# Row maxima of a windowed attention: products over 64 rows of the key and query tiles, or over all 128

## The chip, the cores and the metric

One core of a Trainium2 chip runs the whole program. The metric is device microseconds of one execution, as a median over several runs.

## The reference

The reference is a trunk of two layers on 1024 latent tokens and 256 context tokens of width 1024. Layer 0 is a state-space mixer beside a convolution; layer 1 is a gated MLP beside a windowed attention, and only the latent stream leaves it. What matters here is the attention of layer 1: 16 query heads in 4 groups, each group with one key and value head of 64 channels, blocks of 128 queries, each block against its own and the two neighbouring blocks of keys, the 256 context keys and a sink logit.

```python
qb = jnp.moveaxis(q.reshape(bsz, nb, W, ATT_KV_HEADS, ATT_REP, ATT_HEAD_DIM), 1, 0)
...
s_lat = jnp.einsum('bqkrd,bskd->bkrqs', qblk, kblk).astype(F32) * ATT_SCALE
s_lat = jnp.where(mblk, s_lat, -jnp.inf)
s_ctx = jnp.einsum('bqkrd,bskd->bkrqs', qblk, k_ctx).astype(F32) * ATT_SCALE
s_snk = jnp.broadcast_to(sink_f, s_ctx.shape[:-1] + (1,))
p = jax.nn.softmax(jnp.concatenate([s_lat, s_ctx, s_snk], axis=-1), axis=-1).astype(vblk.dtype)
```

## The kernel before

All products run on TensorE in float32r, with each operand split into a high and a low part (`split`: ScalarE casts the high part, VectorE or GpSimd subtracts for the low part), so most results are three products: high by high, high by low, low by high (`mm3_`, line 170).

The attention (`attention`, lines 476 to 659) goes through 16 units, each one group of heads (`kv`) and one quarter of the queries (`s`, two blocks of 128). A unit has 9 or 10 steps, one for each tile of 128 keys that a block sees. In each step TensorE gets:

- `att_s`, lines 728 and 729: the scores of a key tile for 4 heads into the tile `st`, as two products. The first is over 128 rows: `ks1` holds the keys' high part in rows 0 to 63 and their low part in rows 64 to 127, and `mv1` holds the queries' high part in both halves. The second is over 65 rows, with the queries' low part and, in row 64, the shift that is subtracted from each score. ScalarE then takes exponentials and casts (731, 738), and VectorE or GpSimd makes the low part `pl` (739).
- `att_pv`, line 746: three products of values and exponentials, of the key tile two steps earlier.
- some columns of other work (`beside`): projections of the next groups' queries and gates (line 170), and later the output projection (line 1009), in the order of the string `REST`.
- up to three pieces of `att_max` for the next unit. A piece is a product of queries and keys, and after it VectorE work on the product: pairs of context products of 256 columns with one maximum (lines 686 and 687), and window products of 384 or 256 columns with a masking copy and a maximum (691, 695 or 697, and 698). There are 4 pairs and 8 window products in a unit, 12 pieces.

`att_max` begins by making `mv1` (ScalarE casts, line 672, one for each half of the rows) and `mv2` (VectorE, line 673). When the 12 pieces are done, VectorE joins the maxima (702 to 708), ScalarE takes an exponential (709), TensorE transposes the result (713), and a DMA on GpSimd's queue (716) puts the shift into row 64 of `mv2`, which line 729 of the next unit reads.

Products of `att_max` rotate over three PSUM banks: `ms` twice, and `m2`. The order on TensorE is the order of the program text (`manual_schedule`); the tile framework's scheduler sets the order on the other engines. `fill` (lines 539 to 555) makes `ks1`, `ks2` and `vs` of the next group one unit before the maxima need them; its line 549 is the VectorE subtraction that writes rows 64 to 127 of `ks1`.

The row maximum only shifts the exponent, and it cancels in the softmax; it need not be exact.

Of the kernel before, what the change touches and what calls it, by code (L numbers as in the profile page):

```python
# [11 lines left out]
PSUM = bass.MemoryType.PSUM  # L12
DRAM = bass.MemoryType.DRAM

P = 128
D = 1024
KT = 8
L = 1024
C = 256
T = L + C  # L20
# [69 lines left out]
def run(steps):  # L90
    """Emit a sequence that is emitted in steps."""
    for _ in steps:
        pass
# [6 lines left out]
# What is done on the tensor engine beside the attention, in this order: projections of queries (q) and gates (g) of a group's  # L100
# two head pairs, both halves of the output projection by token tile (c, d) and their weights (R, W, V); @n: from the n-th unit on.
# [4 lines left out]
# Columns of it for each key tile, by unit of the attention.  # L106
# [3 lines left out]
class Kern:  # L110
# [71 lines left out]
    def mod_half(self, layer, i, pool, prio=0):  # L182
        """Half i % 2 of the weight columns (i // 2)*128.., split."""
        return self.load_w(pool, self.A["modw"][layer, i // 2][:, 4 * (i % 2):4 * (i % 2) + 4], [P, 4, P], "m", prio=prio)
# [4 lines left out]
    def mod_chan_(self, layer, m, dst, pool, plus=0.0, halves=1, bank="mm", ahead=None, raw=None, parts=None):  # L189
        """Columns m*128.. of the modulation, channel-major [P, 2] (latents, context)."""  # L190
        nc = self.nc
        n = 8 // halves
        ps = None
        for h in range(halves):
            if ahead is not None:
                w = ahead.pop(0)
                if 2 * m + h + 2 < 32:
                    ahead.append(self.mod_half(layer, 2 * m + h + 2, pool, 300))
            elif halves == 2:
                w = self.mod_half(layer, 2 * m + h, pool)  # L200
            else:
                w = self.load_w(pool, self.A["modw"][layer, m], [P, 8, P], "w", raw=raw, prio=0, parts=parts)
            if ps is None:
                ps = self.bank(bank) if isinstance(bank, str) else bank
            for j in range(2):
                for k in range(n):
                    nc.tensor.matmul(ps[:4, :P], self.scond[:, n * h + k], w[j][:, k], start=(h + j + k == 0), stop=(h + j + k == halves + n - 1))
        yield 1024
        row = self.const.tile([4, P], F32, name="modrow", tag="modrow", bufs=2)
        nc.vector.tensor_copy(row, ps[:4, :P])  # L210
        yield 0
        nc.tensor.matmul(ps[:, 256:258], row, self.V("sel", 0, 2)[:4], start=True, stop=True)
        nc.vector.tensor_scalar(dst, ps[:, 256:258], self.V(f"modb{layer}", m), plus, op0=ALU.add, op1=ALU.add)

    def gate_rows(self, layer, j, dst, bank="ms"):
        """Gate of one stream broadcast over partitions, [P, D]."""
        nc = self.nc
        for f in range(2):
            pt = self.bank(bank)
            for q in range(4):  # L220
                nc.tensor.matmul(pt[:, q * P:(q + 1) * P], self.gcol[:, layer, 4 * f + q, j:j + 1].broadcast_to([P, P]),
                                 self.ident, start=True, stop=True)
            nc.scalar.copy(dst[:, 512 * f:512 * f + 512], pt)
# [143 lines left out]
    def layer1(self, h1, va_d, e0, free_h1):  # L367
        tc, nc, A = self.tc, self.nc, self.A
        dram = self.dram
        hhi, hlo = h1  # L370
        W = A["wch1"]
# [23 lines left out]
        with ExitStack() as e1:  # L395
            q = e1.enter_context(self.pool(name="kv", bufs=2))
            for f in range(2):
                # keys of two heads of the attention, latents and context
                def ev(ps, a, b):
                    t = q.tile([P, 512], F32, name="kt", tag="kt")  # L400
                    if a == 0:
                        nc.scalar.copy(t[:, :b - a], ps)
                    else:
                        self.rope(q, ps, a, b, t)
                    nc.sync.dma_start(kf_d[2 * f:2 * f + 2, :, a:b].rearrange("k d t -> (k d) t"), t[:, :b - a])

                self.proj_ch(wp, W[24 + f], hhi, hlo, ev, pool_lo=f == 1)
                for t in range(8):
                    ps = self.bank("mm")
                    ts = slice(C + t * P, C + (t + 1) * P)  # L410
                    self.mm3(ps, (lambda k: hhi[:, k, ts], lambda k: hlo[:, k, ts]),
                             (lambda k: wv[k // 2][0][:, k % 2], lambda k: wv[k // 2][1][:, k % 2]), range(8))
                    nc.scalar.activation(vt[:, t, 512 * f:512 * f + 512], ps, AF.Gelu_apprx_tanh)
                wv = None if f else load_v(1)
# [9 lines left out]
    def rope(self, q, ps, a, b, out):  # L424
        """Rotated queries or keys of two heads (128 channels), latents a..b."""
# [65 lines left out]
    def attention(self, wp, W, hhi, hlo, kf_d, va_d, yc_d, gd_d, yd_d, den_d, rd_d, sk_d, ew, free_h1):  # L491
        tc, nc, A = self.tc, self.nc, self.A
        LS = SLICES[:2]
        with ExitStack() as e:
# [44 lines left out]
            def fill(kv):  # L539
                """Stationary forms of one group's keys and values."""  # L540
# [20 lines left out]
            def rest():  # L561
                """What fills the tensor engine beside the attention, with the columns of each step; None while there is nothing to do."""
# [98 lines left out]
    def att_max(self, kv, s, qf, KV, out, u, sk_d):  # L661
        """Stationary-side queries of 2 blocks and the shift of each row."""
# [16 lines left out]
        for b in range(2):  # L679
# [3 lines left out]
            for h2 in range(2):  # L683
                ps = self.bank("ms")
                for h in range(2):
                    nc.tensor.matmul(ps[:, 256 * h:256 * h + 256], mv1[0:64, b, 2 * h2 + h], ks1[0:64, 0:C], start=True, stop=True)  # L686
                nc.vector.tensor_reduce(mx[:, 0, b, 2 * h2:2 * h2 + 2], ps.rearrange("p (h k) -> p h k", h=2), axis=mybir.AxisListType.X, op=ALU.max)
                yield
            for h in range(4):
                ps = self.bank("ms")  # L690
                nc.tensor.matmul(ps[:, :nw], mv1[0:64, b, h], ks1[0:64, C + w0 * P:C + w0 * P + nw], start=True, stop=True)  # L691
# [29 lines left out]
    def att_s(self, KV, mv, b, x, kb, off):  # L721
        """Exponentials of the scores of one key tile, 4 heads, split."""
# [9 lines left out]
        if off:  # L732
            # key j of a neighbouring block, query i: kept where i <= j (before) or i >= j (after)
            nc.gpsimd.affine_select(out=p, in_=p, pattern=[[0, 4], [off, P]], base=0, channel_multiplier=-off,
                                    compare_op=ALU.is_ge, fill=0.0)
# [19 lines left out]
    def out1_open(self, yc_d, wr, raws):  # L755
        """Pools and first half of the last output weight."""
# [9 lines left out]
    def out1_c(self, o, t):  # L766
        """The latent stream's residual plus the gated-MLP half of the output projection."""
# [15 lines left out]
    def out1_den(self, q, den_d, rd_d, sk_d, s, h0=0, h1=16):  # L783
        """Reciprocals of twice the softmax denominators, sinks included, of a quarter of the queries, heads h0..h1."""
# [12 lines left out]
    def out1_next(self, o, qp, wr):  # L797
        """Second half of the last output weight."""
# [10 lines left out]
    def out1_y(self, o, q, yd_d, gd_d, rd_d, t0, n, k0, k1, eng):  # L809
        """Gated attention of tokens t0..t0+n (within a quarter), channel tiles k0..k1, split."""  # L810
# [23 lines left out]
    def out1_mm(self, ps, y, w, f, ks, a=0, i0=0):  # L834
        """Channel tiles ks of the product for one half of the channels."""
# [7 lines left out]
    def out1_ln(self, o, x, ps, t):  # L843
        """Residual and the last layer norm."""
# [23 lines left out]
    def out1_d(self, o, q, ten, t, y0):  # L868
        """The attention's half of the output projection of one token tile."""
# [15 lines left out]
    def out1_d67(self, o, q, ten):  # L885
        """The last quarter: the last group's channels come last."""
# [20 lines left out]
    def conformer(self, cv, csum, e):  # L907
        """silu(layer norm over channels) of the convolution, in place."""
# [38 lines left out]
    def split_wo(self, wo, raws, slots, vec=None):  # L947
        """Split one half of an output weight; low parts go to free slots and to those of the values loaded for the tiles before."""
# [17 lines left out]
    def load_wo(self, wo, wr, src, pool_lo=(), more=(), raws=()):  # L966
        """One half (8 K tiles) of an output weight, split; raws are loaded already, the next ones land in the slots of more."""
# [19 lines left out]
    def out_mm(self, ob, src, w, parts=None, by_k=False):  # L987
        """Token tile of an output projection half: two PSUM banks."""
# [23 lines left out]
    def ln_mv(self, q, t):  # L1012
        """mean and rstd over the free dimension."""
# [10 lines left out]
    def ln_stats(self, q, t):  # L1024
        """mean and rstd as scale and bias columns."""
# [118 lines left out]
    def proj_last_(self, wp, src, hhi, hlo, evac, slices, pool_lo=False):  # L1144
        """The low part of the activations is done with first."""
# [22 lines left out]
    def inproj0(self, hhi, hlo, cv, xbc_d, zs_d, gs_d, dtr, vwh, yb_d, xt_d, hb_d, s0, first):  # L1168
# [100 lines left out]
        def token_major(xq, c, h):  # L1269
            """x and B of half a chunk, tokens on partitions."""  # L1270
# [63 lines left out]
    def dt_prep(self, dtr):  # L1334
        """dt, decays and running sums of both directions, [P, dir, chunk, head]."""
        tc, nc, A = self.tc, self.nc, self.A
        cst = self.s0
        with ExitStack() as e:
# [56 lines left out]
            # rows of three exact float32r parts: running sums in head order, biases as (position in quad, quad)  # L1395
# [23 lines left out]
    def ssd_back(self, xt_d, hb_d):  # L1419
        """The state entering each chunk from behind."""  # L1420
# [39 lines left out]
    def rstd_of(self, var, out, scale=1.0):  # L1460
        """out = (var * scale + eps) ** -0.5"""
# [7 lines left out]
class SsdFwd:  # L1469
    """Forward half of the scan and the output of one chunk."""  # L1470
# [6 lines left out]
    def prep(self):  # L1477
        """Loads, the state for the next chunk, C^T B and the diagonal's coefficients."""
# [42 lines left out]
    def mix(self):  # L1521
        """The chunk's output from its own positions and from both states."""
# [43 lines left out]
    def finish(self):  # L1566
        """Gate by z, the RMS statistic, channel-major store."""
# [32 lines left out]
```

## Time and profile before

| | |
|---|---|
| median of 3 runs | 2266.37 us (2262.7 to 2266.95) |
| profiled execution, first to last instruction | 2267.6 us |
| granted TensorE clock, mean of the span | 0.970 |
| attention with its maxima, 1591 to 2107 us | 516 us, of it TensorE busy 502.8, VectorE 319.1, ScalarE 301.0, GpSimd 213.9 |
| from there to the end | 160.6 us, TensorE busy 139.3 |

The profiled execution has no other time than its span; it lies 1.2 us above the median. A row of a timeline gives the start, the duration, the engine, the line, the operation, the names and the shape. In a shape such as `64*128 64x384` the first pair is rows by columns of the array that the weights take, the second is rows by columns of the operand that streams through. Matmuls overlap their neighbours, so the price of one in a stream is the distance from its start to the next one's start, not its duration. PEld is the load of a matmul's weights.

### The profile page before, as it was taken

The page shows a single profiled execution, that of the slowest core. Times are in us where ns is not written, and L with a number is a line of the kernel's source. Part 1 is how long each engine was busy: PE and PEld are TensorE (multiplying, and loading weights), DVE is VectorE, ACT ScalarE, POOL GpSimd, SP SyncE. Part 2 cuts the span into 40 slices and gives each one's busy share as a digit, 9 for nine tenths or more (in the row PEclk, how much of TensorE's full clock was granted, in tenths as well). Part 3 has the DMA queues.
Part 4 walks back from the last instruction along what each step waited for, and adds up shares of the span by engine and source line. Part 5 has one row for each costly group of instructions (what it writes and reads, how often), then busy time and mean ns, then how long its engine had stood idle before and what let it go on. Part 6 is the DMA issues. An engine that isn't in the chain of part 4 may idle for free.

```text
span 2267.6 us, 28582 instructions
## 1 busy us (share of the span) xinstructions
PE 2148.1 (95%) x10748; PEld 1647.3 (73%) x10748; DVE 1470.1 (65%) x1912; ACT 1005.1 (44%) x1553; POOL 1015.7 (45%) x652
## 2 busy tenths in 40 slices
PE   7998998889999999999999999999999999899997
PEld 6877876769997766656789788888666666666676
DVE  6799999988743377677775133223665566566677
ACT  4355565543552233333333233325556666545510
POOL 0088998870223355444330128433344444424453
PEclk9999999989999999899999999999999999899998
DMA  7121111115535765555434224323112111523363
GB/s 271 57 67 57 42 51 64 63 59 170 180 113 191 249 194 176 169 192 180 140 115 134 75 77 170 128 84 98 51 45 60 31 45 53 161 83 116 111 187 128
DMA packets 160145, 262.79 MB, mean 116 GB/s; under 512 B 19028, under 2 KB 98768, under 8 KB 159752
## 3 DMA queue, kind: packets, MB, share of 16 engines
q1 hardware_dynamic: 158584, 257.45, 34.9%
q0 software_dynamic: 1280, 3.26, 0.5%
q8 instruction: 84, 1.38, 0.2%
q14 instruction: 53, 0.43, 0.1%
q10 hardware_dynamic: 144, 0.26, 0.0%
HBM read 186.55 MB, written 74.32 MB: 115 GB/s over the span
## 4 chain that ended last, share of the span: by engine, by line
PE 58%; DVE 7%; DMA 5%; ACT 3%; issue 2%; POOL 2%; SPq 0%; POOLq 0%; DVEq 0%; ACTq 0%
PE m L170 28%; PE m L1009 12%; PE po L746 4%; PE st L728 2%; PE st L729 1%; PE ms L691 1%; DMA mr<-in_modw_dram 1%; PE m L840 1%; PE po L1542 1%; DVE ml L158 1%; PE ms L686 1%; ACT rb L433 1%; POOL ks L828 1%; PE m L691 1%; PE yd L1563 1%
## 5 line engine op out<-in xcount | busy, mean ns | idle before, releaser
L170 PE MATMUL m<-hhi,wh 128*128 128x512 f32 (+1 forms) x840 | 306.9, 369 | 36.8 <-ACT pad L1235 35.2
L1216 POOL TENSOR_TENSOR accq<-accq,prod 128x1295 f32<-128x1295 f32 x90 | 319.0, 3545 | 43.7 <-ACT prod L1215 30.3
L170 PE MATMUL m<-hlo,wh 128*128 128x512 f32 (+1 forms) x840 | 308.2, 367 | 0.0
L170 PE MATMUL m<-hhi,wl 128*128 128x512 f32 (+1 forms) x840 | 306.1, 365 | 1.0 <-DVE wl L158 1.0
L1224 DVE SCALAR_TENSOR_TENSOR acc<-u,vwh,acc 128x1295 f32<-128x1295 f32 x150 | 234.8, 1565 | 6.1 <-issue 2.2
L739 POOL TENSOR_TENSOR pl<-pt,ph 128x512 fp32r<-128x512 f32 x96 | 129.0, 1344 | 236.7 <-ACT ph L738 227.7
L170 PE MATMUL m<-h1hi,wh 128*128 128x512 f32 (+1 forms) x544 | 218.3, 401 | 2.0 <-ACT rb L433 1.4
L170 PE MATMUL m<-h1lo,wh 128*128 128x512 f32 (+1 forms) x544 | 217.0, 399 | 0.0
L170 PE MATMUL m<-h1hi,wl 128*128 128x512 f32 (+1 forms) x544 | 216.3, 398 | 0.0
L170 PEld LDWEIGHTS m<-hhi,wh 128*128 128x128 f32 x840 | 161.7, 194 | 64.4 <-ACT pad L1235 38.3
L1009 PE MATMUL m<-woh,yh 128*128 128x512 f32 x448 | 187.0, 421 | 0.6 <-ACT yh L157 0.2
L1009 PE MATMUL m<-wol,yh 128*128 128x512 f32 x448 | 185.3, 414 | 1.0 <-DVE wol L158 0.5
L1009 PE MATMUL m<-woh,ylo 128*128 128x512 f32 x448 | 185.0, 413 | 0.5 <-DVE ylo L158 0.5
L170 PEld LDWEIGHTS m<-hhi,wl 128*128 128x128 f32 x840 | 162.6, 194 | 27.9 <-issue 3.4
L170 PEld LDWEIGHTS m<-hlo,wh 128*128 128x128 f32 x840 | 163.0, 194 | 24.6 <-issue 2.4
L1215 ACT ACTIVATE prod<-u,vwh 128x1295 f32<-128x1295 f32 x90 | 123.4, 1378 | 82.0 <-POOL accq L1216 81.9
L738 ACT CAST ph<-pt 128x512 fp32r<-128x512 f32 x152 | 93.1, 619 | 115.3 <-PE po L746 107.9
L158 POOL TENSOR_TENSOR wl<-wr,wh 128x1024 fp32r<-128x1024 f32 x33 | 80.6, 2443 | 122.7 <-ACT wh L157 99.0
L1244 DVE SCALAR_TENSOR_TENSOR acc<-pad,vecs,acc 128x1282 f32<-128x1282 f32 x48 | 131.8, 2748 | 3.2 <-issue 1.8
L170 PEld LDWEIGHTS m<-h1hi,wh 128*128 128x128 f32 x544 | 103.2, 190 | 28.7 <-issue 2.6
L746 PE MATMUL po<-ph,vs 128*66 128x512 f32 x304 | 122.9, 404 | 0.8 <-ACT ph L738 0.8
L731 ACT ACTIVATE pt<-st 128x512 f32<-128x512 f32 x152 | 90.7, 597 | 74.2 <-PE st L729 54.5
(360 smaller groups left out, 4890.2 us busy)
## 6 DMA issues: line engine op xcount, KB each, us to landing
wr<-in_wch_dram SPq DMA_DIRECT2D x69, 512.0 KB
mr<-in_modw_dram SPq DMA_DIRECT2D x64, 256.0 KB
mr<-in_modw_dram SPq DMA_DIRECT2D x16, 512.0 KB
wor<-in_wout_dram SPq DMA_DIRECT2D x16, 512.0 KB
xcT<-xbc_d SPq DMA_DIRECT2D x20, 320.0 KB
xt_d<-xtok SPq DMA_DIRECT2D x20, 320.0 KB
xtok<-xt_d SPq DMA_DIRECT2D x10, 640.0 KB
xt<-xt_d SPq DMA_DIRECT2D x10, 640.0 KB
```

The lines of the kernel that those rows point to most:

```text
L158: (nc.gpsimd if pool_lo else nc.vector).tensor_tensor(lo, src, hi.bitcast(F32), op=ALU.subtract)
L170: nc.tensor.matmul(out, x(k), y(k), start=(c == 0), stop=(c == tot - 1))
L691: nc.tensor.matmul(ps[:, :nw], mv1[0:64, b, h], ks1[0:64, C + w0 * P:C + w0 * P + nw], start=True, stop=True)
L731: nc.scalar.activation(p.rearrange("p h t -> p (h t)"), ps, AF.Exp, scale=0.125)
L738: nc.scalar.copy(ph, p)
L739: (nc.gpsimd if x in (0, 1, 3) else nc.vector).tensor_tensor(pl, p, ph.bitcast(F32), op=ALU.subtract)
L746: nc.tensor.matmul(po[:66], vs[:, kb, v], p[y], start=first and i == 0, stop=last and i == 2)
L1009: nc.tensor.matmul(ps[f], y[u][:, k], w[k][v][:, 512 * f:512 * f + 512], start=i + j == 0, stop=i + j == 9)
L1215: nc.scalar.activation(pr, u[:, k:k + N], AF.Copy, scale=vwh[:, i, k:k + 1])
L1216: nc.gpsimd.tensor_tensor(acc, acc, pr, op=ALU.add)
L1224: nc.vector.scalar_tensor_tensor(acc[:, :N], u[:, k:k + N], vwh[:, i, k:k + 1], acc[:, :N], op0=ALU.mult, op1=ALU.add)
L1244: nc.vector.scalar_tensor_tensor(acc, pad[:, k:k + N], w(k), acc, op0=ALU.mult, op1=ALU.add)
```

## The change

Both products of `att_max` use all 128 partitions of `mv1` and `ks1` instead of the first 64. The product is then of the queries' high part with the keys' high and low parts together. The rest of the diff removes comments and docstrings.

```diff
-                    nc.tensor.matmul(ps[:, 256 * h:256 * h + 256], mv1[0:64, b, 2 * h2 + h], ks1[0:64, 0:C], start=True, stop=True)
+                    nc.tensor.matmul(ps[:, 256 * h:256 * h + 256], mv1[:, b, 2 * h2 + h], ks1[:, 0:C], start=True, stop=True)
...
-                nc.tensor.matmul(ps[:, :nw], mv1[0:64, b, h], ks1[0:64, C + w0 * P:C + w0 * P + nw], start=True, stop=True)
+                nc.tensor.matmul(ps[:, :nw], mv1[:, b, h], ks1[:, C + w0 * P:C + w0 * P + nw], start=True, stop=True)
```

The order on TensorE and on SyncE's queue is the same in both kernels. The scheduler places some instructions differently on VectorE (in five places), on ScalarE (two) and on GpSimd (one). On VectorE, in the middle of one unit's maxima (masking copies 697, maxima 698, beside them the rotation of projected queries, 434), the difference is:

```order
 L697 COPY_PREDICATED m_14916<-mk,low 128x2x128
 L739 TENSOR_TENSOR pl<-pt,ph 128x512
-L697 COPY_PREDICATED ms<-mk,low 128x2x128
 L698 TENSOR_REDUCE mxs<-m_14916 128x1
-L698 TENSOR_REDUCE mxs<-ms 128x1
-L434 TENSOR_TENSOR rb<-rb,rope 128x512
+L697 COPY_PREDICATED ms<-mk,low 128x2x128
+L434 TENSOR_TENSOR rb<-rb,rope 128x512
+L698 TENSOR_REDUCE mxs<-ms 128x1
```

The masking copy of one product moves behind the maximum of the product before it, and the rotation moves ahead of the next maximum.

On VectorE at the head of another unit's maxima (context maxima 687 beside a low part of exponentials, 739) it is:

```order
 L739 TENSOR_TENSOR pl<-pt,ph 128x512 x2
 L673 TENSOR_TENSOR mv_16665<-qf,mv_16664 64x2x128 x4
-L687 TENSOR_REDUCE mxs<-ms 128x2
-L739 TENSOR_TENSOR pl<-pt,ph 128x512
-L687 TENSOR_REDUCE mxs<-ms 128x2
+L739 TENSOR_TENSOR pl<-pt,ph 128x512
+L687 TENSOR_REDUCE mxs<-ms 128x2 x2
```

The low part goes ahead of the first context maximum instead of between the two.

## Rows read from the trace of the kernel before

**Rows 1.** The page, part 1: busy us, share of the span, instructions.

```profile
PE 2148.1 (95%) x10748; PEld 1647.3 (73%) x10748; DVE 1470.1 (65%) x1912; ACT 1005.1 (44%) x1553; POOL 1015.7 (45%) x652
```

**Rows 2.** Waits of PE, 1590 to 2120 us: us in total, times, longest us.

```profile
PE ms L713 <- ACT mpack L709: 2.7, 1, 2.7
PE po L746 <- DVE pl L739: 2.5, 3, 2.0
PE ms L686 <- ACT mv L672: 1.3, 3, 0.5
```

**Rows 3.** Lines 686 and 691: times, ns min/median/max, first and last start, shapes.

```profile
L686 PE MATMUL ms<-ks,mv x88: 271/379/579, 1591.4 to 2101.1; 64*128 64x256 f32 x88
L686 PE MATMUL m<-ks,mv x40: 271/380/579, 1621.1 to 2061.8; 64*128 64x256 f32 x40
...
L691 PE MATMUL ms<-ks,mv x84: 379/437/686, 1595.2 to 2105.3; 64*128 64x384 f32 x64, 64*128 64x256 f32 x20
L691 PE MATMUL m<-ks,mv x44: 380/437/686, 1594.0 to 2106.3; 64*128 64x384 f32 x32, 64*128 64x256 f32 x12
```

**Rows 4.** Timeline of PE around a context pair: start us, us, instruction.

```profile
1811.61 0.40 PE L729 MATMUL st<-mv,ks 65*128 65x512 f32 x1
1811.85 0.40 PE L170 MATMUL m<-h1hi,wl 128*128 128x512 f32 x1
1812.18 0.49 PE L686 MATMUL ms<-ks,mv 64*128 64x256 f32 x2
1812.60 0.50 PE L170 MATMUL m<-h1hi,wh 128*128 128x512 f32 x1
1812.94 0.39 PE L170 MATMUL m<-h1lo,wh 128*128 128x512 f32 x1
```

**Rows 5.** Timeline of PE around a window product.

```profile
1816.20 0.39 PE L170 MATMUL m<-h1hi,wl 128*128 128x512 f32 x1
1816.53 0.44 PE L691 MATMUL ms<-ks,mv 64*128 64x384 f32 x1
1816.90 0.50 PE L170 MATMUL m<-h1hi,wh 128*128 128x512 f32 x1
1817.23 0.39 PE L170 MATMUL m<-h1lo,wh 128*128 128x512 f32 x1
```

**Rows 6.** Timeline of PE where full-height products of 256 columns follow each other.

```profile
1230.43 0.28 PE L170 MATMUL m<-wvh,h1lo 128*128 128x256 f32 x1
1230.55 0.28 PE L170 MATMUL m<-wvh,h1hi 128*128 128x256 f32 x1
```

**Rows 7.** VectorE by line and shape, 1590 to 2110 us: busy us, mean ns | idle before.

```profile
L698 DVE TENSOR_REDUCE mxs<-ms 128x1 f32<-128x384 f32 x64 | 34.6, 550 | 0.6
L697 DVE COPY_PREDICATED_SCALAR ms<-mk,low 128x256 f32 x64 | 30.9, 484 | 16.0 <-PE ms L691 14.9
L687 DVE TENSOR_REDUCE mxs<-ms 128x2 f32<-128x512 f32 x44 | 30.2, 685 | 15.6 <-PE ms L686 15.5
```

**Rows 8.** Seven of 16 units, first to last product of the maxima, and the sum of 16. Columns: stretch, its us, busy us (and count) of PE, PEld, DVE, ACT, POOL, granted clock, DMA share, GB/s.

```profile
1591.06:1605.99 14.93, 14.93 (x52) 8.28 (x51) 12.88 (x28) 8.76 (x17) 5.31 (x4) 1.00 0.41 116
...
1647.74:1664.97 17.23, 17.02 (x59) 9.21 (x58) 14.57 (x25) 9.21 (x18) 6.18 (x6) 1.00 0.22 69
...
1741.51:1765.61 24.10, 23.05 (x59) 12.01 (x58) 14.58 (x27) 13.32 (x26) 7.55 (x6) 0.72 0.13 31
1778.76:1796.72 17.96, 17.37 (x59) 9.43 (x58) 14.62 (x27) 12.99 (x24) 8.40 (x7) 1.00 0.14 38
...
1873.23:1891.49 18.26, 17.38 (x59) 9.16 (x57) 14.96 (x29) 13.13 (x28) 6.34 (x5) 1.00 0.18 46
...
2051.99:2070.39 18.40, 18.40 (x67) 10.45 (x65) 14.72 (x29) 7.95 (x14) 4.15 (x5) 1.00 0.22 67
2088.80:2106.94 18.14, 18.14 (x66) 10.38 (x65) 16.61 (x31) 8.12 (x16) 8.30 (x7) 1.00 0.40 127
sum 290.37, PE 282.43 PEld 157.71 DVE 217.68 ACT 157.44 POOL 97.16; mean PE 17.65 PEld 9.86 DVE 13.61 ACT 9.84 POOL 6.07
```

## The prediction

> **What bounds the kernel now.** I read the page first: TensorE is busy for 95% of the span, VectorE for 65%, the others for under half [rows 1]. The change touches only products of the attention's maxima, so the next view is the waits of TensorE in that stage. In some 520 us its waits for other engines come to a few microseconds: 2.7 at the first unit's transpose, 2.5 for low parts of exponentials, 1.3 for the queries' casts [rows 2]. TensorE bounds this stage, and a microsecond taken from its stream there is a microsecond of the span until another engine becomes the bound. What follows the attention (the output projection's last part) waits for the attention's end, so it shifts and does not shrink.
>
> Being busy says nothing about whether the stream is dense, so I then read starts in the timeline, around a product of each touched kind. In a plain stretch one product of 512 columns starts 0.23 to 0.24 us after the one before it; the 65-row product of the scores does so too, from 1811.61 to 1811.85 [rows 4]. Full-height products of 256 columns start 0.12 us apart [rows 6]. Around a pair of 64-row products it is different: from the plain product at 1811.85 to the pair it takes 0.33 us, the pair takes 0.42, and the plain product behind it needs 0.34 until the next starts [rows 4]. A window product alone shows the same: 0.33, 0.37, 0.33 [rows 5]. So TensorE pays on the way into the 64-row products, in them, and on the way out.
>
> **The change, part by part.**
>
> *Height of the products.* It takes 256 products in 192 visits: 128 context products in 64 pairs (88 and 40) and 128 window products (84 and 44) [rows 3]; 12 visits in each of 16 units. The price of a visit comes from the starts. The pair: 1812.94 - 1811.85 = 1.09 us [rows 4]. The same columns at full height and plain spacing: 0.23 + 0.12 + 0.12 + 0.23 = 0.70. Difference 0.39. The window product: 1817.23 - 1816.20 = 1.03 us [rows 5]; plain, with 384 columns halfway between 256 and 512, 0.23 + 0.175 + 0.23 = 0.64. Difference again 0.39. If full height removes the whole difference, TensorE's stream gets shorter by 192 x 0.39 = 75 us, 4.7 us in each unit.
>
> Does full height remove it? The trace of before has no full-height product at this place, but its neighbours bound it. Rows of 128 and of 65 both run at plain spacing [rows 4], so it is not the height as an amount of work, nor a wait on a semaphore as such: the score product also waits for others and costs nothing extra. From below, the gain is nothing if the loads of these weights are slow for another reason; from above it is 75. I take the whole 75, because the new products have the very operands of line 728 (`mv1` and `ks1`, 128 rows), with their roles swapped.
>
> [...]
>
> *What VectorE lets through.* Each piece asks VectorE for a context maximum (685 ns) or a masking copy and a maximum (484 + 550 ns) [rows 7]. With TensorE 4.7 us faster in a unit, VectorE may not follow. In the 16 stretches from first to last product VectorE is busy for 217.7 of 290.4 us [rows 8]. Unit by unit, a stretch cannot become shorter than VectorE's work in it, unless that work runs on past the last product. The room (stretch minus VectorE) is under 4.7 us by a clear margin in six units: 2.1, 2.7, 3.3, 3.3, 3.7 and 1.5 us, in the order of the rows, with 1741.51 left out [rows 8]. Those six give 16.6. The ten others at 4.7 give 47. Together 63.6 us. That is the sum if nothing trails; 75 is the sum if all of VectorE's surplus trails into the stretch after the last product, where TensorE has about as much time again before the next unit and VectorE has little to do. Three PSUM banks let a product run ahead of VectorE by up to three pieces, so some of it will trail. I take 66.
>
> *The new waits.* The products now also wait for the second half of `mv1` (one more cast, line 672, in front of a pair) and for `ks1`'s low half (line 549). The first is bounded by nothing (the casts are done when TensorE arrives) and by one cast for each of 16 units at what the existing wait costs now, up to 0.5 us each [rows 2], 8 us. TensorE waits there only 3 times today, so I take 1 us. Behind a waiting product stand the scores and the value products of the running unit, as TensorE goes in order. The second I take at nothing: `fill` runs one unit ahead of the maxima, and in the first unit the products read the context keys first; if that cover were gone, it would be one subtraction once in each of four groups.
>
> *The order on VectorE.* The moved copies, maxima and rotations are the same instructions; they cost nothing while VectorE has room. A low part that stands behind a maximum can make the value products wait, as it does for 2.5 us now [rows 2]. That is why I stay well below 75.
>
> Sum: 66 - 1 = 65 us less. The profiled execution has 2267.6 us, the median is 1.2 lower; 2267.6 - 65 - 1.2 = **2201 us**.
>
> **The rivals.**
>
> *VectorE takes half of it back.* If VectorE's work packs badly, each unit ends with about 2 us in which TensorE waits for it (a masking copy and a maximum of the last pieces, 2 x 1.03 us [rows 7]). Then 16 x 2 = 32 us fall off the 63.6, less 1 for the casts: gain 30, time 2235. For it: six units where VectorE has hardly room [rows 8]. Against it: VectorE idles for 15 us each before lines 687 and 697, waiting for TensorE [rows 7], which a faster TensorE gives back.
>
> *More than the sum.* One unit ran at a granted clock of 0.72 and took 24.1 us where its like take 17 to 18 [rows 8]. If that stretch, some 6.5 us, is not repeated and all of the 75 comes, with up to 4 us of the small waits [rows 2] gone, the gain is about 85 and the time 2181.
>
> *Nothing changes.* If the extra time belongs to the place (weights that change at each product, banks that are freed late) and not to the height, the starts stay as they are and the time is 2266. For it: nothing in the starts but that no full-height product stands exactly there. Against it: rows 4. [...]
>
> [...]
>
> **How the numbers follow.** Forecast (gain 55 to 78) 0.68; half taken back 0.13; more than the sum 0.13; nothing 0.04; slower 0.02. The likeliest is 2201. The range reaches from 2180 (more than the sum) to 2235 (half taken back) and leaves out nothing, slower and the far ends of these two, some 0.15. A measurement of this kernel can tell 0.2% from no change, 4.5 us. Faster by more than that: 0.94, within it 0.04, slower 0.02.
>
> **What would show it.** Right: starts around a visit at plain spacing (0.23, 0.12 or about 0.18), 16 stretches that sum to about 225 us instead of 290, VectorE busy for 90% and more of them, small new waits of TensorE on lines 687, 697, 698 and 739, and an unchanged 160 us behind the attention. Wrong on the height: distances of 0.33 and 0.37 stay. Wrong on VectorE: distances are plain, but waits of 1 us and more stand before lines 686 and 691. Wrong on the clock: stretches below 0.9 granted clock in more than two units.

## The result, and the profile after

The changed kernel takes 2207.45 us (median of 4 runs, 2205.72 to 2211.47) against 2264.53 of the kernel before (4 runs, 2257.74 to 2266.95): ratio 0.9754, 95% interval 0.9727 to 0.9781, 57 us faster. The forecast was 2201, in a range from 2180 to 2235. The profiled execution has a span of 2203.9 us, 63.7 less than the one before. Part of that difference is the granted clock of the execution profiled before (0.970): of 31 further runs of that kernel the four at a mean granted clock of 0.979 or more took 2255.5 to 2258.7 us, the three at 0.971 or less 2266.7 to 2271.1.

The whole forecast hung on the starts of TensorE's products. Here is the timeline of TensorE in the changed kernel around a context pair and around a window product, the same places of the program as [rows 4, 5]:

```profile
1781.22 0.40 PE L729 MATMUL st<-mv,ks 65*128 65x512 f32 x1
1781.45 0.40 PE L170 MATMUL m<-h1hi,wl 128*128 128x512 f32 x1
1781.68 0.40 PE L686 MATMUL ms<-ks,mv 128*128 128x256 f32 x2
1781.92 0.40 PE L170 MATMUL m<-h1hi,wh 128*128 128x512 f32 x1
1782.16 0.39 PE L170 MATMUL m<-h1lo,wh 128*128 128x512 f32 x1
...
1784.65 0.40 PE L170 MATMUL m<-h1hi,wl 128*128 128x512 f32 x1
1784.88 0.34 PE L691 MATMUL ms<-ks,mv 128*128 128x384 f32 x1
1785.06 0.40 PE L170 MATMUL m<-h1hi,wh 128*128 128x512 f32 x1
1785.29 0.39 PE L170 MATMUL m<-h1lo,wh 128*128 128x512 f32 x1
```

The distances were 0.33, 0.42 and 0.34 us around the pair and are now 0.23, 0.24 and 0.24; around the window product 0.33, 0.37 and 0.33 became 0.23, 0.18 and 0.23. Twice as many rows are multiplied, and the 0.39 us extra of a visit are gone to a hundredth or two.

The loads of the weights (PEld) show where these 0.39 us sat. The first three lines are the loads around the window product of [rows 5] in the kernel before, the last is the load of the window product above in the changed kernel:

```profile
1816.53 0.18 PEld L691 LDWEIGHTS ms<-ks,mv 64*128 64x128 f32 x1 [0.36 <-DVE ms L697]
1816.89 0.19 PEld L170 LDWEIGHTS m<-h1hi,wh 128*128 128x128 f32 x1 [0.19 <-issue]
1817.00 0.19 PEld L170 LDWEIGHTS m<-h1lo,wh 128*128 128x128 f32 x1
...
1784.65 0.19 PEld L691 LDWEIGHTS ms<-ks,mv 128*128 128x128 f32 x1
```

In the changed kernel the load starts together with the product before its own (1784.65) and runs under it; its own product starts at 1784.88. At a change of height it does not: the load for the 64-row product starts only with that product (1816.53), and so does the load for the first 128-row product behind it (1816.89, the product at 1816.90). In the trace of before this is so at all 192 ways into a visit and all 192 ways out; in the changed kernel 393 of the 448 loads at these places start with the product before, the others later, most of them where TensorE waits. The profile puts the idle time before the first load down to VectorE's copies (697), but the changed kernel has the same copies and no such time. Two loads of 0.18 to 0.19 us in the open are about the price of a visit. That they are its cause is argued from their places and sizes: no run changed a load alone.

Next, the 16 stretches from first to last product of a unit's maxima, columns as in [rows 8], the same seven units and the sum of 16:

```profile
1592.28:1604.00 11.72, 10.99 (x52) 8.39 (x51) 11.59 (x26) 8.80 (x17) 5.11 (x3) 1.00 0.42 117
...
1640.03:1654.14 14.11, 12.60 (x59) 9.48 (x58) 13.51 (x23) 9.13 (x18) 5.52 (x5) 1.00 0.22 65
...
1722.23:1737.57 15.34, 12.72 (x60) 9.48 (x58) 12.85 (x25) 12.57 (x24) 7.21 (x6) 1.00 0.21 49
1751.53:1766.27 14.74, 13.16 (x59) 9.56 (x58) 13.25 (x24) 12.83 (x24) 7.87 (x6) 1.00 0.09 18
...
1834.78:1850.18 15.40, 12.95 (x59) 9.28 (x57) 14.13 (x28) 12.41 (x27) 6.63 (x5) 1.00 0.21 54
...
1993.97:2008.22 14.25, 14.00 (x66) 10.88 (x65) 13.62 (x27) 7.97 (x14) 3.89 (x5) 1.00 0.22 57
2027.91:2044.07 16.16, 14.59 (x66) 10.37 (x65) 15.90 (x30) 8.14 (x16) 7.58 (x6) 1.00 0.47 142
sum 225.29, PE 206.09 PEld 157.74 DVE 201.51 ACT 152.34 POOL 91.41; mean PE 12.88 PEld 9.86 DVE 12.59 ACT 9.52 POOL 5.71
```

The stretches went from 290.4 to 225.3 us, 65.1 less. VectorE is now busy for 201.5 of 225.3 us, 89%; it was 75% before. What lies between these stretches took 225.5 us before and takes 226.5 now, and what follows the attention 160.7 and 159.8: nothing was gained or lost there. So the change acted in the maxima and nowhere else.

Last, what TensorE waits for in this stage (1590 to 2060 us; us in total, times, longest), all waits of 1 us and more:

```profile
PE po L746 <- DVE pl L739: 5.5, 5, 2.0
PE m L221 <- DVE gdt L533: 5.0, 1, 5.0
PE ms L686 <- ACT mv L672: 4.9, 8, 1.1
PE po L746 <- POOL pl L739: 4.5, 4, 1.7
PE ms L713 <- ACT mpack L709: 2.7, 1, 2.7
PE m L691 <- DVE mxs L698: 1.7, 5, 0.7
PE po L746 <- ACT ph L738: 1.7, 2, 1.2
PE m L170 <- ACT rb L433: 1.4, 1, 1.4
PE m L713 <- ACT mpack L709: 1.3, 2, 0.7
```

Beside the three lines of [rows 2] the kernel before had a wait of 0.8 us for exponentials (738) and these two, the first of them the longest of its stage:

```profile
PE m L221 <- DVE gdt L533: 4.7, 1, 4.7
PE po L746 <- POOL pl L739: 0.9, 2, 0.6
```

The wait for VectorE's low parts grew from 2.5 to 5.5 us, that for the queries' casts from 1.3 to 4.9, that for GpSimd's low parts from 0.9 to 4.5; waits of line 691 for a bank are new, and the wait of line 221 stays as it was. All of TensorE's waits in the stage come to 12.9 us before and 29.6 now; by the engine that ended last, VectorE's grew by 5.7 us, ScalarE's by 7.4 and GpSimd's by 3.6. VectorE's side shows the reverse (busy us, mean ns | idle before):

```profile
L697 DVE COPY_PREDICATED_SCALAR ms<-mk,low 128x256 f32 x64 | 30.0, 477 | 2.2 <-PE ms L691 2.0
L687 DVE TENSOR_REDUCE mxs<-ms 128x2 f32<-128x512 f32 x44 | 29.9, 682 | 3.5 <-PE ms L686 3.2
```

Its idle time before these two lines was 16.0 and 15.6 us [rows 7] and is 2.2 and 3.5. There TensorE hardly keeps it waiting any more.

### The profile page after: what moved, and what is told of

Its sections match the earlier page's. It is cut to its first block, busy times and chain, and to the rows that moved or that the text cites. A ratio compares the mean times of both kernels' runs of the same rounds, so it can differ in the third digit from the quotient of the medians.

```text
span 2203.9 us, 28585 instructions
## 1 busy us (share of the span) xinstructions
PE 2060.6 (93%) x10748; PEld 1637.6 (74%) x10748; DVE 1467.6 (67%) x1912; ACT 1002.4 (45%) x1553; POOL 1016.9 (46%) x652
## 4 chain that ended last, share of the span: by engine, by line
PE 52%; DVE 10%; DMA 5%; ACT 5%; issue 3%; POOL 2%; SPq 0%; POOLq 0%; DVEq 0%; ACTq 0%
PE m L170 25%; PE m L1009 11%; PE po L746 3%; PE st L729 1%; PE st L728 1%; PE po L1542 1%; PE m L840 1%; ACT rb L433 1%; ACT mv L672 1%; DVE ml L158 1%; DMA mr<-in_modw_dram 1%; PE sg L1553 1%; POOL ks L828 1%; PE yd L1563 1%; DMA vs<-rd_d 1%
## 5 line engine op out<-in xcount | busy, mean ns | idle before, releaser
L170 PE MATMUL m<-h1hi,wh 128*128 128x512 f32 (+1 forms) x544 | 212.6, 391 | 1.9 <-ACT rb L433 1.4
L170 PE MATMUL m<-h1hi,wl 128*128 128x512 f32 (+1 forms) x544 | 211.8, 390 | 0.0
L170 PEld LDWEIGHTS m<-h1hi,wl 128*128 128x128 f32 x544 | 102.4, 188 | 21.0
```

The source lines that it names most:

```text
L170: nc.tensor.matmul(out, x(k), y(k), start=(c == 0), stop=(c == tot - 1))
```

## The experiments

**One row more than 64.** The products use 65 rows, without the other 63 rows of the keys' low part.

```diff
-    nc.tensor.matmul(ps[:, :nw], mv1[:, b, h], ks1[:, C + w0 * P:C + w0 * P + nw], start=True, stop=True)
+    nc.tensor.matmul(ps[:, :nw], mv1[0:65, b, h], ks1[0:65, C + w0 * P:C + w0 * P + nw], start=True, stop=True)
```

(and the context products likewise)

> The maxima's products use rows 0 to 64 (65 rows) instead of all 128, so the keys' low part is left out but for one channel. Theory (a product of more than 64 rows is issued as a full-height one, and only the height counts): starts around a visit at 0.23, 0.12 and 0.18 us, the time within 6 us of the changed kernel's 2207. Rival (what counts is how much of the array is filled, or what the products compute): distances near those of 64 rows, a time near 2264. Rival (the new placement on VectorE made the gain): the distances stay long and the time goes with VectorE's order.

2206.89 us (4 runs), ratio 0.9746, interval 0.9727 to 0.9766: the same as at 128 rows. The timeline around a pair:

```profile
1778.79 0.40 PE L746 MATMUL po<-ph,vs 128*66 128x512 f32 x1
1779.02 0.41 PE L686 MATMUL m<-ks,mv 65*128 65x256 f32 x2
1779.27 0.40 PE L170 MATMUL m<-h1lo,wh 128*128 128x512 f32 x1
```

Starts are 0.23 and 0.25 us apart. What the other 63 rows compute plays no part; 65 rows are enough. The sum of the 16 stretches is 225.05 us, against 225.3 at 128 rows. The rival that VectorE's new order made the gain is not settled by this run; the kernel before without masking copies (below) leaves it no room, as 58 us less of VectorE's work gain nothing there.

**Half of the change, either half.** First the window products alone at full height (line 691), then the context pairs alone (line 686).

```diff
 # e2: of the kernel before, line 691 alone
-    nc.tensor.matmul(ps[:, :nw], mv1[0:64, b, h], ks1[0:64, ...], start=True, stop=True)
+    nc.tensor.matmul(ps[:, :nw], mv1[:, b, h], ks1[:, ...], start=True, stop=True)
 # e3: of the kernel before, line 686 alone
-    nc.tensor.matmul(ps[:, ...], mv1[0:64, b, 2 * h2 + h], ks1[0:64, 0:C], start=True, stop=True)
+    nc.tensor.matmul(ps[:, ...], mv1[:, b, 2 * h2 + h], ks1[:, 0:C], start=True, stop=True)
```

> Only the 128 window products have full height; the 64 context pairs keep 64 rows. Theory (0.39 us a visit, each visit on its own): two thirds of the visits go, 50 of 75 us in TensorE's stream, and two thirds of the measured 57 us in the time, 2226. Rival (VectorE bounds the maxima and takes the rest): alone the window products meet less of the limit, so more than two thirds comes, 45 us or more, 2219 or less, and the two halves add up to clearly more than 57.

> Only the 64 context pairs have full height; the window products keep 64 rows. Theory (each visit on its own): one third of 57 us, 2245. Rival (VectorE bounds the maxima): 22 us or more, 2242 or less, and the sum with the other half is clearly more than 57 us. Neighbouring visits of both kinds (a pair, one plain product, a window product) should each keep or lose their own 0.39 us.

Window products alone: 2228.42 us, ratio 0.9843 (0.9822 to 0.9865). Context pairs alone: 2239.14 us, ratio 0.9892 (0.9865 to 0.9919). Against 2264.27 of the kernel before on the same chip these are 36 and 25 us. The two halves together give 61, the whole change 57. The intervals are some 5 us wide to each side, so the theory's 38 and 19 and the rival's "clearly more than 57" are not told apart by these times; the window products' 36 us fall short of the rival's 45, the pairs' 25 exceed its 22. The 16 stretches sum to 243.6 and 265.6 us, against 290.4 before and 225.3 with both: 46.8 and 24.8 less alone, 65.1 together and not 71.6. Half of these 6.5 us of overlap is the clock: the unit of [rows 8] at a granted clock of 0.72 counts its loss in both halves (5.5 us), and one stretch of the first half ran at 0.89 (2.4 us the other way). The 14 other units overlap by 3.3 us, as they must if other engines begin to hold TensorE up. In a unit that nothing else holds, the parts add up. This is the unit at 1811.85, which took 16.54 us before and takes 11.86 with both, with the window products alone and with the pairs alone at full height:

```profile
1789.26:1802.65 13.39, 13.39 (x59) 9.32 (x58) 10.67 (x23) 8.59 (x16) 6.05 (x5) 1.00 0.23 70
1793.86:1808.85 14.99, 14.99 (x59) 9.39 (x58) 10.97 (x23) 8.70 (x16) 6.61 (x6) 1.00 0.20 62
```

3.15 and 1.55 us less are eight and four visits at 0.39, and both together take off 4.68. The units at 1712.12 and 2018.90 show the same to 0.05 us.

**Twice the product in one visit.** The kernel before with each window product issued twice; the output is the same.

```diff
     nc.tensor.matmul(ps[:, :nw], mv1[0:64, b, h], ks1[0:64, C + w0 * P:C + w0 * P + nw], start=True, stop=True)
+    nc.tensor.matmul(ps[:, :nw], mv1[0:64, b, h], ks1[0:64, C + w0 * P:C + w0 * P + nw], start=True, stop=True)
```

> The kernel before with each 64-row window product issued twice in a row, with the same result. It prices what happens inside a visit. Theory (only the change of height costs, on the way in and out): the second product starts some 0.18 us after the first, the time grows by 128 x 0.18 = 23 us. Rival (between 64-row products the weights are not loaded under the running product either, as 0.42 us for a pair lets one think): 0.28 us, 36 us.

The timeline around one such visit (line numbers behind 691 are one higher):

```profile
1815.51 0.39 PE L170 MATMUL m<-h1hi,wl 128*128 128x512 f32 x1
1815.84 0.44 PE L691 MATMUL ms<-ks,mv 64*128 64x384 f32 x1
1816.12 0.33 PE L692 MATMUL ms<-ks,mv 64*128 64x384 f32 x1
1816.38 0.50 PE L170 MATMUL m<-h1hi,wh 128*128 128x512 f32 x1
1816.71 0.40 PE L170 MATMUL m<-h1lo,wh 128*128 128x512 f32 x1
```

The second product does start 0.28 us after the first, as the rival said, but the next plain product then follows 0.26 us behind and not 0.37. From 1815.51 to 1816.71 it is 1.20 us; a visit with one product took 1.03 [rows 5]. The second product adds 0.17 us, its plain price. In all 96 visits with products of 384 columns the two distances are these to 0.01 us. In sum the theory holds: the visit has a price, not the product. The time, one run of 2275.25, is 11 us above the kernel before where 23 were expected; the runs of the kernel before beside it lie 9 us apart, so a single run prices nothing, and the starts decide.

**Fewer visits, the same products.** If that is so, the kernel before can be helped at 64 rows: two window products next to each other, so that their 128 visits become 64.

```diff
     nc.vector.tensor_reduce(mx[:, 1, b, h:h + 1], ps[:, :nw], axis=mybir.AxisListType.X, op=ALU.max)
-    yield
+    for _ in range(2 * (h % 2)):
+        yield
```

> The kernel before, all products at 64 rows, but the window products issued two and two next to each other: 64 visits fewer, the same products. Theory (a visit costs 0.39 us whatever is in it, for the two changes of height): 64 x 0.39 = 25 us less, 2240. Rival (each 64-row product pays for itself, because its weights are not loaded under a running product): starts of 0.28 to 0.37 us for each, at most 6 us gained.

2240.32 us (4 runs), ratio 0.9887 (0.9863 to 0.9912), 24 us faster than 2264.05 of the kernel before beside it. This is the cleanest test of the price in the time: no product changed its height, none was left out, and 64 visits fewer gave 24 us where 25 were expected and the rival allowed 6. The interval reaches from 20 to 31 us, so that they agree to 1 us is luck. The pieces come in other steps of a unit, so the order of TensorE's work shifts a little and the stretches cannot be set against those of before. In its trace 128 visits are left, and a visit with two products of 384 columns has the distances of the one above (0.33, 0.28, 0.26 and 0.33 us).

**VectorE relieved, at either height.** The masking copies are left out, so the row maxima are taken over the whole window.

```diff
-    a, n = int(w0 == B), (w0 < B) + (w1 > B)
-    edge = ps[:, :P] if w1 == B else ...
-    if n == 1:
-        nc.vector.copy_predicated(out=edge, mask=mk[:, a], data=self.low.broadcast_to([P, P]))
-    else:
-        nc.vector.copy_predicated(out=edge, mask=mk, data=self.low.unsqueeze(2).broadcast_to([P, 2, P]))
     nc.vector.tensor_reduce(mx[:, 1, b, h:h + 1], ps[:, :nw], axis=mybir.AxisListType.X, op=ALU.max)
```

> The changed kernel (128 rows) without the masking copies of the maxima (lines 693 to 697): the row maximum is then taken over the whole window, masked keys included, which only shifts the exponent. VectorE loses 96 x 0.48 + 32 x 0.35 = 58 us of work, TensorE nothing. Theory (what the 16 stretches of maxima still have above TensorE's plain 196 us, 225 - 196 = 29, is mostly VectorE): the stretches fall to about 208 us and the time by 12 to 18 us, to 2192. Rival (the casts of the queries on ScalarE, or the chain of exponentials, hold the rest): less than 5 us, 2203 or more.

> The same without masking copies in the kernel before (64 rows). Theory (there TensorE's bubbles bound the maxima and VectorE had room): nothing to gain, within 5 us of 2264, while the same edit gains 12 to 18 at 128 rows. Rival (VectorE's work costs the same in both): the same gain as at 128 rows, 2250.

At 128 rows 2197.08 us (5 runs), ratio to the kernel before 0.9696 (0.9672 to 0.9719), where the changed kernel, run once more (below), has 0.975 (0.9728 to 0.9771): some 10 to 12 us faster than the changed kernel. At 64 rows 2262.06 us (10 runs), ratio 0.9982 (0.996 to 1.0003), no difference that the runs can tell; 12 of its 16 stretches are the same as before to 0.1 us. So VectorE holds a part of the maxima at 128 rows and none at 64. But the gain is under the 12 to 18 expected. The sum of the stretches and the waits of TensorE in the stage at 128 rows without masks (line numbers behind 691 are six lower):

```profile
sum 218.97, PE 203.75 PEld 159.32 DVE 167.86 ACT 148.74 POOL 89.29; mean PE 12.73 PEld 9.96 DVE 10.49 ACT 9.30 POOL 5.58
```

```profile
PE ms L686 <- ACT mv L672: 4.8, 8, 1.1
PE po L740 <- POOL pl L733: 4.7, 4, 2.2
PE m L221 <- DVE gdt L533: 4.7, 1, 4.7
PE po L740 <- ACT ph L732: 3.6, 2, 2.4
PE po L740 <- DVE pl L733: 2.5, 4, 1.1
```

Three of the six units that had little room, those at 1640.03, 1751.53 and 1834.78 in the changed kernel:

```profile
1631.15:1645.23 14.08, 12.55 (x60) 9.55 (x59) 11.84 (x18) 9.15 (x18) 5.53 (x5) 1.00 0.23 66
1740.84:1755.14 14.30, 12.89 (x60) 9.62 (x58) 11.44 (x19) 12.39 (x24) 7.96 (x6) 1.00 0.07 13
1823.61:1838.47 14.86, 12.66 (x58) 9.35 (x57) 12.03 (x22) 11.88 (x26) 6.11 (x5) 1.00 0.21 56
```

VectorE falls to 168 us in the stretches, the stretches only from 225 to 219 and not to 208. The waits for VectorE's low parts go from 5.5 to 2.5 us, those of line 691 from 1.9 to 0.2, and the one for the transpose (line 713, 4.0 us) is gone; those for ScalarE's casts and for GpSimd's low parts stay. The three units had 14.11, 14.74 and 15.40 us and lose 0.0, 0.4 and 0.5, although VectorE now has 2 to 3 us to spare in each: something else held them, and in these three TensorE waits for the queries' casts, 0.7, 1.4 and 1.7 us with the masking copies and 0.7, 1.4 and 1.6 without. What the stretches have above TensorE's own 196 us (an estimate: the columns of their products at 0.23 us for 512) is thus VectorE's for a part only. The rest is a mixture of ScalarE, GpSimd and the one wait of line 221, which stood there before the change.

**The second cast, on another engine.** Twice: on GpSimd, in the changed kernel, and on VectorE, in the kernel without masks.

```diff
-    for r in range(2):
-        nc.scalar.copy(mv1[64 * r:64 * r + 64, :, 2 * i + hh], src)
+    nc.scalar.copy(mv1[0:64, :, 2 * i + hh], src)
+    nc.gpsimd.tensor_copy(mv1[64:128, :, 2 * i + hh], src)   # e9: nc.vector
```

> The changed kernel with the second half of the queries' tile (rows 64 to 127) cast by GpSimd instead of ScalarE, 64 casts of 0.42 us taken off ScalarE. It is about the new wait: context pairs now wait for both halves, and waits on line 672 went from 1.3 to 4.9 us. Theory (the second cast in front of the pair is the wait): these waits go back to about 1 us, the time to 2203. Rival (GpSimd's casts stand behind its low parts of 1.3 us, and the pair waits for them instead): the wait moves to GpSimd, the time stays or is some us longer, 2207 to 2213.

> The 128-row kernel without masking copies, and the second half of the queries' tile cast by VectorE, which has the room now, instead of ScalarE: 27 us of work change sides. Theory (in the units with the longest stretches, 14 to 15 us, ScalarE is busy for 12 to 13 and holds TensorE at line 672): the waits on line 672 go from 4.8 to 2 us or less, the sum of the stretches from 219 to about 213, the time to 2191. Rival (the chain of exponentials holds these units, not the casts): waits move to line 746, the time stays at 2197 or more.

On GpSimd 2215.53 us (4 runs, 2212.08 to 2221.95), ratio 0.9783 (0.9754 to 0.9812): some 8 us slower than the changed kernel, and beyond what either side expected. The wait of the pairs did go, from 4.9 us to 0.7 on GpSimd's cast:

```profile
sum 233.50, PE 212.33 PEld 162.79 DVE 208.73 ACT 127.92 POOL 106.33; mean PE 13.27 PEld 10.17 DVE 13.05 ACT 8.00 POOL 6.65
```

```profile
PE po L746 <- DVE pl L739: 9.8, 6, 2.7
...
PE ms L686 <- POOL mv L672: 0.7, 2, 0.4
```

The stretches are 8 us longer all the same: VectorE is busier by 7 us for the same instructions (its subtraction for `mv2` takes 700 ns on average instead of 606), and its low parts come later. There is a second reason, which this run does not separate from the first: five stretches of its profile have a granted clock of 0.83 to 0.90, where the changed kernel has one below full clock. The two that grew most, by 3.3 and 2.5 us, both stand at 0.90. On VectorE it is 2206.17 us, ratio 0.9735 (0.9711 to 0.9759), 9 us slower than without that move. The waits on line 672 are gone here too, but the sum of the stretches is 225.4 us, not 213. One row tells much of why; line, operation and shape, busy us, mean ns | idle before:

```profile
L672 DVE CAST mv<-qf 64x256 fp32r<-64x256 f32 x60 | 38.9, 649 | 18.7 <-PE st L722 17.2
```

VectorE stands still for 17 us before these casts, until the scores of the unit before have read the buffer that they write, and the maxima queue behind it: line 691 now waits for context maxima, 4.0 and 3.6 us, and line 746 for VectorE's low parts 5.8 instead of 2.5. Four of its stretches were granted 0.89 to 0.96, against two at 0.93 and 0.95 without the move, so here too the clock has a part that is not separated. In this kernel the casts are better off on ScalarE, by some 8 and 9 us, although TensorE waits for them.

**The changed kernel once more.**

> The changed kernel once more, beside the kernels above on the same chip, so that the gains are taken from runs of one place: 2207, ratio 0.975.

2206.9 us (5 runs), ratio 0.975 (0.9728 to 0.9771), and 223.6 us for the sum of the stretches. The fastest kernel of the study is the one without masking copies at 128 rows, 2197.08 us.

## Why the prediction was right

**Height of the products: right.** 192 visits at 0.39 us, 75 us of TensorE's stream, were said to go whole, and the distances are now plain ones in the pair, in the window product and behind both. That the price belongs to the visit is shown three ways: 65 rows pay nothing (2206.89 us), two products in a visit pay once (the second adds 0.17 us), and with 64 visits fewer the time falls by 24 us. What the prediction left open ("if the loads of these weights are slow") is answered by the loads: they are no slower than others (0.18 to 0.19 us), but at all 384 changes of height in the trace of before they start with their own product, where in a plain stretch they start 0.23 us ahead of it.

**What VectorE lets through: right in the sum, only partly in the cause.** The unit-by-unit sum was 63.6 us, the forecast 66 less 1. The profiles' stretches differ by 65.1. The six units with little room were given 16.6 us and gained 18.5 (3.2, 3.1, 3.2, 2.9, 4.2 and 2.0); the ten others were given 47 and gained 46.6. Four things behind these numbers were not as argued. Four of the ten others had less room than 4.7 us too (4.3, 4.0, 4.2 and 4.4), so the rule taken strictly gives 61.7. VectorE's work did run on past the last products, as I had supposed: between the stretches it is busy for 110.8 us instead of 101.3, and these took 226.5 us instead of 225.5, so it cost next to nothing. 8.8 of the 46.6 come from one unit, the one at a granted clock of 0.72 before and at full clock after; without its 4 us above the price of twelve visits the ten others would have stayed at 42.5.

And VectorE was not the engine that held most of the rest: without its masking copies three of the six units with little room kept 14.1, 14.3 and 14.9 of their 14.1, 14.7 and 15.4 us. What is missing from 75 is the 17 us by which TensorE's waits grew, 7.4 of them for ScalarE, 5.7 for VectorE and 3.6 for GpSimd (1.3 of ScalarE's, at the transpose, hang on VectorE's maxima, as the run without masks shows): 75 and some 6.5 of the unit at low clock, less 17, are 64 or 65. That a bound on VectorE alone came out there too is in good part luck; in two of the units with little room ScalarE is busy for most of the stretch as well (12.8 of 14.7 us and 12.4 of 15.4, from 1751.53 and 1834.78).

**The new waits: the term that was mis-sized.** One microsecond was taken for the second cast in front of a pair, from a range up to 8. The wait on line 672 went from 1.3 to 4.9 us. For `fill` nothing was taken, and no wait for line 549 shows. GpSimd's low parts (0.9 to 4.5 us) were not in the sum at all: the text looked for late low parts on VectorE only.

**From the profile to the median.** The profiles differ by 63.7 us, the medians by 57. The forecast was made against a profiled execution of 2267.6 us that contained the unit at low clock just named, and corrected it by 1.2 us to the median of three runs. But a run's time lies 1.8 to 2.0 us above its core's span, so that execution stands for some 2269.4 us, 5 above the median of its kernel and above all four runs; the one profiled after has 2205.72, 2 below its median. That is the difference between 63.7 and 57. The runs of the kernel before seen since lie between 2255 and 2271, those of the changed kernel between 2202 and 2211. The 6 us between 2201 and 2207 lie within these spreads; the 31 runs of the kernel before are on the whole shorter the higher their granted clock, and the profile that the sum was made on was taken at the low end of it.

**The rivals.** "Nothing changes" fell with the first timeline. "Slower", a granted clock that falls in unit after unit as it did in the stretch from 1741.51 before (0.72), did not happen: 15 of 16 stretches were granted 1.00, the other 0.93. "VectorE takes half of it back" had too high a price, and only in part the right engine: 2 us a unit were feared, and 65 of 75 us came through. The 75 us of TensorE's stream did come whole: the 0.2 us in the middle of a visit are paid once for each visit too, like the way in and the way out, as a second product in it adds its plain 0.17 us.

## What to carry to other kernels

A visit of 64-row products in a stream of full-height ones costs 0.39 us here, whether it holds one product or two: fill the operands up if they have the rows (65 were enough, 2206.89 us against 2207.45 with 128), or put such products next to each other. Read starts against starts in the timeline, and the starts of the loads beside them, before believing a TensorE that is 95% busy. And before counting such a gain, ask of every engine that feeds TensorE, not only of the busiest one, what it will be waited for: the sum over VectorE alone (63.6) came near the profiles (65), but more of the new waiting was for ScalarE (7.4 us) than for VectorE (5.7).

## What the runs showed of the hardware

By the starts of the products, a visit of 64-row products costs 0.10 us on the way in, about 0.2 us once within, and 0.11 us behind it; a second product of 384 columns adds its plain 0.17 us. Products of 65 rows started at the spacing of 128 (0.23 and 0.25 us around a pair, against 0.23 and 0.24). At each of the 384 changes of height in the trace of before the recorded start of the product is that of its load to 0.01 us, where a plain stretch has 0.23 us between them, so the three parts are not to be read one by one: what is shown is their sum, 0.39 us for going in and out. I had not expected the price to hang on the visit alone, so closely that it forecasts another kernel (25 us less expected, 24 measured, interval 20 to 31).

In the kernel before, one unit's stretch fell to a granted clock of 0.72 in the profile (0.50 for some 13 us; from 1747.0 to 1759.9 plain products of 512 columns, one behind the other, start 0.42 to 0.43 us apart instead of 0.23), and in the 64-row kernel without masks the same unit to 0.62 and 27 us; with the window products doubled it had 0.85. In both profiles of the changed kernel, at 65 rows, and with either half or the paired visits it did not fall (1.00); with the second cast on another engine it had 0.89. Ahead of the fall TensorE had stood idle for 0.77 and 0.28 us, waiting for exponentials and a low part. The same place of the changed kernel has longer idle time (TensorE busy for 0.78 of the 2 us from 1724) at full clock, so that wait alone does not bring it. Each of these is a single profile; why that unit, and whether the visits had a part in it, stays open.
